# A decoder layer on one core: a rearranged head of the run, with more dense warm-up products

## The chip, the cores and the metric

The kernel runs on one core of a Trainium2 chip. The metric is the device time of one execution in microseconds, from runs of the same program; the median is compared. Of TensorE's clock two levels occur in this document, 1.2 and 2.4 GHz, called half and full.

## The reference

For one sequence of 256 tokens with 1024 channels the layer computes, all in float32:

```
mod = silu(c) @ w_ada + b_ada              # shift, scale, gate, 1024 each
h   = rmsnorm(x, norm_g) * (1 + scale) + shift
proj = h @ w_in                            # q, k, v, g_attn, cb, cc, cx, g_conv, m_attn, m_conv
attn = moba_attention(q, k, v, rel_bias)   # SEQ = MOBA_BLOCK: plain causal attention of 8 heads
y_attn = (attn * silu(g_attn)) @ w_o_attn
y_conv = (cb * conv3(cc * cx) * silu(g_conv)) @ w_o_conv
merged = sigmoid(m_attn) * y_attn + sigmoid(m_conv) * y_conv
out = rmsnorm(x + gate * (merged @ w_out), final_g)
```

Only the first two lines, and the beginning of the third, lie in the part that is changed.

## The kernel before, in words

**The head.** `x` is loaded as two tiles of 128 tokens into `xx[:, 0]` and `xx[:, 1]`, and `c` as one row, `crow`. A product with `ones` spreads `c` over 128 partitions (`pc`, L225, two products of 512 columns, contraction over one row). ScalarE and VectorE make silu(c) of it, `csb` (`silu_part`, L231). The modulation is not computed on TensorE: `w_ada` comes transposed, 128 channels to a tile `ada`, and VectorE multiplies each tile with `csb` and sums along the row (`ada_dot`, L148; the sums go to `parts`, the finished shift and scale of the 128 channels to `scs`). Meanwhile each tile of `x` is squared and summed on ScalarE (`square`, L236), `rms_scale` (L141) makes the inverse root of it (VectorE, then a power on GpSimd, `r0` and `r1`), ScalarE scales the tile, TensorE transposes it in 16 blocks of 128x128 into four banks `px` (`xn_trans`), and four copies bring them to `xnT` (`xn_copy`). `full_h(0)` (ScalarE) applies `scs` to the first 128 channels of `xnT` and gives `hf0`, the first operand of the large products.

**The stream of products.** For the k-tiles 0 to 7 (128 input channels each) `passes` (L196) multiplies a slab of `w_in` (`slab`, 2048 columns of q and k, loaded in two halves) with h, into eight banks `acc`. For k-tile 0 all 16 products are native float32, `hf0` by `slab0`, two records in the trace each. For the later ones slab and h are mostly split into a high and a low part of a faster type (`slab1h`, `slab1l`, `H`) by ScalarE and VectorE, and three products take the place of one native one. From there on the kernel goes through v, attention, convolution, gates and output in the same manner.

**What sets the order.** Nearly every instruction of the head is pinned in program order (`pin`), so each engine works its list strictly from top to bottom, and a wait holds up everything behind it on that engine. Loads go out on one queue, SyncE's, in the order of the code; the small `vecs` (norm_g, biases) and `onehot` loads go out on GpSimd's. `warm(n)` (L137) issues n products of 128x128 `ones` by `ones` whose result nobody reads.

Of the kernel before, what the change touches and what calls it, by code (L numbers as in the profile page):

```python
# [23 lines left out]
EPS = 1e-6
NEG = -1.0e30
BLK = {n: i * D for i, n in enumerate(("q", "k", "v", "ga", "cb", "cc", "cx", "gc", "ma", "mc"))}
WARM = 4
WARM2 = 6
EARLYC = 2
HALF = 8  # L30
AHEAD = 3
VCUT = 640
NATIVES = [16, 4, 2, 2, 2, 2, 2, 0]
CUTS0 = (0, 2, 3, 4)
CUTS = (0, 2, 4)
UNITS = ([("ada", i) for i in range(KT)] + [("gate", i) for i in range(4)]
         + [("v", n, kh) for n in range(2) for kh in range(2)]
# [6 lines left out]
def layer_kernel(ctx: ExitStack, tc, x, c, vec, wp_all, slab_all, onehot, final_g, out):  # L44
    nc = tc.nc
    x, out = x[0], out[0]

    const = ctx.enter_context(tc.tile_pool(name="const", bufs=1))
    big = ctx.enter_context(tc.tile_pool(name="big", bufs=1))
    wp = ctx.enter_context(tc.tile_pool(name="wp", bufs=3))  # L50
    tp = ctx.enter_context(tc.tile_pool(name="tp", bufs=2))
# [25 lines left out]
    pin = tc.keep_in_program_order  # L77
# [4 lines left out]
    xx = big.tile([P, 4, D], F32, tag="GA", name="xx")  # L82
    xnT = big.tile([P, KT, S], F32, tag="BI", name="xnT")
    csb = big.tile([P, D], F32, tag="AG", name="csb")
    crow = big.tile([1, D], F32, tag="GB", name="crow")
    vecs = const.tile([56, P], F32, name="vecs")
    oneh = const.tile([32, 3 * P + NH], F32, name="oneh")
    ident = const.tile([P, P], F32, name="ident")
    ones = const.tile([P, P], F32, name="ones")
    mhalf = const.tile([P, 1], F32, name="mhalf")  # L90
    vT = const.tile([P, 56], F32, name="vT")
    rv = const.tile([NH, 3 * P], F32, name="rv")
    scs = const.tile([P, KT, 2], F32, name="scs")
    parts = const.tile([P, KT, 2, 5], F32, name="parts")
# [18 lines left out]
            load_ada(i + 1, CUTS)  # L113
        load_slab(i, 1)

    pin(nc.sync.dma_start(crow, c))
    pin(nc.sync.dma_start(xx[:, 0, :], x[0:P, :]))
    pin(nc.sync.dma_start(xx[:, 1, :], x[P:2 * P, :]))
    load_ada(0, CUTS0)
    for h in range(2):  # L120
        load_slab(0, h)
    load_ada(1, CUTS)
    for i in range(1, AHEAD):
        load_ktile(i)
# [5 lines left out]
    nc.gpsimd.dma_start(oneh, onehot)  # L130
    nc.gpsimd.memset(rv[:, 0:127], NEG)
    warmup = const.tile([P, 1], F32, name="warmup")
    pin(nc.scalar.activation(warmup, mhalf, AF.Sigmoid))

    wt = bank("wt")

    def warm(n):  # L137
        for _ in range(n):
            pin(nc.tensor.matmul(wt[:, 0:P], ones, ones, start=True, stop=True))  # L139

    def rms_scale(ss, name):  # L141
        ms = tp.tile([P, 1], F32, tag="ms", name=name + "m")
        pin(nc.vector.tensor_scalar(ms, ss, 1.0 / D, EPS, op0=ALU.mult, op1=ALU.add))
        r = tp.tile([P, 1], F32, tag="rs", name=name + "r")
        nc.gpsimd.tensor_tensor(r, ms, mhalf, op=ALU.pow)
        return r
# [63 lines left out]
    def xn_trans(t, k):  # L210
        c0 = (k % 2) * S + t * P
        pin(nc.tensor.transpose(px[k // 2][:, c0:c0 + P], xx[:, 2 + t, k * P:(k + 1) * P], ident))

    def xn_copy(g):
        dst = xnT[:, 2 * g:2 * g + 2, :].rearrange("p a b -> p (a b)")
        if g % 2 == 0:
            pin(nc.scalar.activation(dst, px[g], AF.Copy))
        else:
            pin(nc.vector.tensor_copy(dst, px[g]))

    ss = tp.tile([P, 2], F32, name="ss")
    warm(WARM)
    pc = [bank(f"pc{n}") for n in range(2)]
    for n in range(2):
        pin(nc.tensor.matmul(pc[n], ones[0:1, :], crow[:, n * 512:(n + 1) * 512], start=True, stop=True))  # L225
    pv = bank("pv")
    pin(nc.tensor.transpose(pv[:, 0:56], vecs, ident[0:56, 0:56]))
    px = [bank(f"px{g}") for g in range(4)]
# [2 lines left out]
    def silu_part(n):  # L231
        cols = slice(n * 512, (n + 1) * 512)
        pin(nc.scalar.activation(csb[:, cols], pc[n], AF.Sigmoid))
        pin(nc.vector.tensor_mul(csb[:, cols], csb[:, cols], pc[n]))

    def square(t):  # L236
        pin(nc.scalar.activation(xx[:, 2 + t, :], xx[:, t, :], AF.Square, accum_out=ss[:, t:t + 1]))

    silu_part(0)
    square(0)  # L240
    r0 = rms_scale(ss[:, 0:1], "r0")
    pin(nc.vector.tensor_copy(vT, pv[:, 0:56]))
    modb = vT[:, 8:24].rearrange("p (k s) -> p k s", s=2)
    pin(nc.vector.scalar_tensor_tensor(modb[:, :, 1], modb[:, :, 1], 1.0, vT[:, 0:KT], op0=ALU.add, op1=ALU.mult))
    pin(nc.vector.tensor_copy(parts[:, :, :, 4], modb))
    silu_part(1)
    square(1)
    dot = ada_dot(0, CUTS0, 256)
    run(dot, EARLYC)
    r1 = rms_scale(ss[:, 1:2], "r1")  # L250
    run(dot)
    pin(nc.scalar.activation(xx[:, 2, :], xx[:, 0, :], AF.Copy, scale=r0))
    for k in range(2):
        xn_trans(0, k)
# [202 lines left out]
    n = 0  # L457
    for j in range(4):
# [7 lines left out]
        for t in range(2):  # L466
# [102 lines left out]

    def finish(t, ms, cols, src=None):  # L570
        r = tp.tile([P, 1], F32, tag="rs", name=f"rf{t}")
        nc.gpsimd.tensor_tensor(r, ms, mhalf, op=ALU.pow)  # L572
        pregain(t, cols, src)
        nc.vector.tensor_scalar_mul(TT[:, t, 0:VCUT], TT[:, t, 0:VCUT], r)
        nc.sync.dma_start(out[t * P:(t + 1) * P, 0:VCUT], TT[:, t, 0:VCUT])
        nc.scalar.activation(TT[:, t, VCUT:], TT[:, t, VCUT:], AF.Copy, scale=r)
        nc.scalar.dma_start(out[t * P:(t + 1) * P, VCUT:], TT[:, t, VCUT:])

    for n in range(2):
# [10 lines left out]
        else:  # L590
# [5 lines left out]
            ms = tp.tile([P, 1], F32, tag="ms", name="ms0")  # L596
# [78 lines left out]
```

## Time and profile before

| what | us |
|---|---|
| median of 3 runs | 329.48 |
| lowest, highest | 328.32, 330.96 |
| profiled execution, span from first to last instruction | 329.4 |
| TensorE busy | 321.4 (98%) |
| VectorE busy | 247.3 (75%) |
| ScalarE busy | 189.0 (57%) |

For the profiled execution the page gives no time beside its span. Times in the rows are microseconds from the start of the span, durations "mean" or min/median/max in ns. PE is TensorE, PEld its loads of the stationary operand, DVE VectorE, ACT ScalarE, POOL GpSimd, SPq SyncE's queue of loads. The column PEclk is the granted clock as a share of full speed. It needs care here: the trace holds a first clock record some 19 us after the start, and ahead of it the column stands at 1.00 whatever the clock was.

### The profile page before, as it was taken

Reading aid. Unit: us, or ns where it says so; the run is one execution under the profiler, and the core shown is the slowest. Engines: PE = TensorE matmul, PEld = TensorE weight load, DVE = VectorE, ACT = ScalarE, POOL = GpSimd, SP = SyncE. Lnnn points to the kernel's source line nnn. Section 1 sums busy time; section 2 is a strip of 40 time slices with the busy share of each in tenths; the row PEclk is TensorE's granted clock in tenths of the full one; section 3 lists DMA queues with packets and bytes.
Section 4 is the critical chain, followed back from the end, with each engine's and each line's share of the span. In section 5 each row is a group of like instructions: output and inputs, shape, how many; then the busy total and the mean of one; then the engine's idle time right before and its main releaser. Section 6 shows DMA issues by size and latency. Waiting matters only on the chain.

```text
span 329.4 us, 4903 instructions
## 1 busy us (share of the span) xinstructions
PE 321.4 (98%) x1870; PEld 281.9 (86%) x1870; DVE 247.3 (75%) x452; ACT 189.0 (57%) x305; POOL 5.6 (2%) x14
## 2 busy tenths in 40 slices
PE   8999999999999999999999999999999999999992
PEld 5689999988888888988888888888888888888892
DVE  2799993476388779697776998999946466787764
ACT  5654555364578676784768574856465635443430
POOL 3000000000000000000000000000000000000010
PEclk9999999999999999999999999999999999999998
DMA  6999999885645434543454469659875665400003
GB/s 240 406 409 403 410 412 352 309 303 214 247 150 200 171 129 141 211 160 127 137 206 169 142 217 373 225 193 370 346 294 205 228 218 202 182 0 2 0 0 127
DMA packets 14264, 72.75 MB, mean 221 GB/s; under 512 B 1523, under 2 KB 2819, under 8 KB 8098
## 3 DMA queue, kind: packets, MB, share of 16 engines
q1 hardware_dynamic: 12658, 70.40, 57.4%
q10 hardware_dynamic: 1488, 1.97, 1.9%
q8 instruction: 14, 0.23, 0.3%
q0 software_dynamic: 96, 0.09, 0.1%
q14 instruction: 8, 0.07, 0.1%
HBM read 71.39 MB, written 1.06 MB: 220 GB/s over the span
## 4 chain that ended last, share of the span: by engine, by line
PE 93%; DMA 2%; DVE 2%; ACT 1%; POOL 1%; SPq 0%; issue 0%; POOLq 0%; DVEq 0%; ACTq 0%
PE acc L205 15%; PE aoa L340 5%; PE acx L340 5%; PE aoc L340 5%; PE acb L340 5%; PE agc L340 5%; PE aga L340 4%; PE amc L340 4%; PE ama L340 4%; PE acc L340 4%; PE aoc L341 2%; PE aoa L341 2%; PE acx L341 2%; PE acc L341 2%; PE acb L341 2%; PE amc L341 2%
## 5 line engine op out<-in xcount | busy, mean ns | idle before, releaser
L205 PE MATMUL acc<-hf,slab 128*128 128x256 f32 x60 | 16.1, 418 | 0.0
L205 PEld LDWEIGHTS acc<-hf,slab 128*128 128x128 f32 x60 | 12.2, 213 | 3.0 <-ACT H L270 1.3
L155 DVE CUSTOM_DVE_ANT_0 ada<-ada,csb,vT 128x512 f32<-128x512 f32 (+1 forms) x18 | 12.3, 687 | 0.0
L155 DVE CUSTOM_DVE_ANT_0 ada<-ada,csb 128x512 f32<-128x512 f32 (+1 forms) x18 | 11.2, 626 | 0.5 <-DMA ada<-in_wp_dram 0.5
L407 DVE CUSTOM_DVE_ANT_0 L<-pS,BI 128x128 f32<-128x128 f32 x8 | 2.3, 292 | 12.2 <-PE pS L404 12.2
L306 DVE TENSOR_SCALAR QK<-acc 128x512 f32<-128x512 f32 x2 | 1.4, 686 | 9.1 <-PE acc L205 9.1
L572 POOL TENSOR_TENSOR rf<-ms,mhalf 128x1 f32<-128x1 f32 x2 | 1.7, 826 | 306.1 <-DVE ms L597 302.5
L554 ACT ACTIVATE SQ<-TT 128x512 f32<-128x512 f32 x3 | 1.9, 626 | 7.6 <-DVE TT L549 7.6
L304 ACT ACTIVATE QK<-acc 128x512 f32<-128x512 f32 x4 | 2.2, 601 | 7.0 <-PE acc L205 7.0
L377 DVE CUSTOM_DVE_ANT_0 gate<-gate,csb,vT 128x512 f32<-128x512 f32 x8 | 6.0, 744 | 0.3 <-DMA gate<-in_wp_dram 0.3
L139 PE MATMUL wt<-ones 128*128 128x128 f32 x20 | 5.0, 437 | 1.0 <-DVE parts L127 1.0
L340 PE MATMUL aoa<-GA,oa0h 128*128 128x512 f32 x16 | 5.8, 404 | 0.0
L340 PE MATMUL aoa<-GA,oa1h 128*128 128x512 f32 x16 | 5.7, 399 | 0.0
L340 PE MATMUL aoc<-GC,oc2h 128*128 128x512 f32 x16 | 5.7, 399 | 0.0
L340 PE MATMUL aoc<-GC,oc1h 128*128 128x512 f32 x16 | 5.7, 399 | 0.0
L340 PE MATMUL aoa<-GA,oa3h 128*128 128x512 f32 x16 | 5.7, 399 | 0.0
L340 PE MATMUL acx<-H,cx0h 128*128 128x512 f32 x16 | 5.7, 398 | 0.0
L340 PE MATMUL aoc<-GC,oc0h 128*128 128x512 f32 x16 | 5.7, 398 | 0.0
L340 PE MATMUL aoa<-GA,oa2h 128*128 128x512 f32 x16 | 5.7, 398 | 0.0
L340 PE MATMUL aoc<-GC,oc3h 128*128 128x512 f32 x16 | 5.7, 398 | 0.0
L340 PE MATMUL acc<-H,cc0h 128*128 128x512 f32 x16 | 5.7, 398 | 0.0
L340 PE MATMUL acb<-H,cb0h 128*128 128x512 f32 x16 | 5.7, 398 | 0.0
(460 smaller groups left out, 1221.9 us busy)
## 6 DMA issues: line engine op xcount, KB each, us to landing
slab<-in_slab_dram SPq DMA_DIRECT2D x16, 512.0 KB, 10.2
ada<-in_wp_dram SPq DMA_DIRECT2D x15, 512.0 KB, 10.2
wv<-in_wp_dram SPq DMA_DIRECT2D x4, 1024.0 KB, 10.6
wcc<-in_wp_dram SPq DMA_DIRECT2D x4, 1024.0 KB, 4.8
wcx<-in_wp_dram SPq DMA_DIRECT2D x4, 1024.0 KB, 4.8
wcb<-in_wp_dram SPq DMA_DIRECT2D x4, 1024.0 KB, 4.8
wgc<-in_wp_dram SPq DMA_DIRECT2D x4, 1024.0 KB, 4.8
wga<-in_wp_dram SPq DMA_DIRECT2D x4, 1024.0 KB, 4.9
```

Source lines behind the costliest of these rows:

```text
L139: pin(nc.tensor.matmul(wt[:, 0:P], ones, ones, start=True, stop=True))
L155: pin(nc.vector.tensor_tensor_reduce(src, src, csb[:, k:k + n], vT[:, i:i + 1] if s else 1.0, 0.0, ALU.mult, ALU.add, parts[:, i, s, k // ...
L205: pin(nc.tensor.matmul(acc[j // 2][:, (j % 2) * S:(j % 2 + 1) * S], w[i][:, j * P:(j + 1) * P], x, start=(i == 0 and j // 2 not in opened) ...
L304: pin(nc.scalar.activation(dst, src, AF.Copy, scale=scale))
L306: pin(nc.vector.tensor_scalar_mul(dst, src, scale))
L340: nc.tensor.matmul(a, hi[:, k, cols], rhs[:, k, :], start=(k == 0), stop=False)
L341: nc.tensor.matmul(a[:, S:], lo[:, k, cols], rhs[:, k, 0:S], start=False, stop=(k == KT - 1))
L377: nc.vector.tensor_tensor_reduce(src, src, csb[:, q * 512:(q + 1) * 512], 1.0, 0.0 if q else vT[:, 24 + b:25 + b], ALU.mult, ALU.add, gpar ...
L407: nc.vector.tensor_tensor_reduce(L[:, 0:P], pS[:, 0:P], BI[:, h, 0:P][:, ::-1], 1.0, -3.0e38, ALU.add, ALU.max, mx[:, 0:1])
L554: nc.scalar.activation(SQ[:, t, 0:w], TT[:, t, cols], AF.Square, accum_out=s8[:, slot:slot + 1])
L572: nc.gpsimd.tensor_tensor(r, ms, mhalf, op=ALU.pow)
```

## The change

- Loads: `x` tile 0, then `c`, then `x` tile 1 (before: `c`, `x`, `x`). `crow` becomes a tile of 128 rows that is zeroed first (its first half on VectorE, its second on GpSimd), and `c` is loaded into row 0 behind that. The product that spreads `c` contracts over 128 rows.
- The first `ada` tile is loaded in two parts, not three, and its dots have 512 columns (4 of them), not 256 (8).
- Warm-up products: 11 at the beginning (before 4), 6 in the middle as before, and 6 new ones right ahead of the first product with `slab0`.
- Squares: tile 0 stays on ScalarE, and comes ahead of the first sigmoid; tile 1 goes to VectorE. Both sums then go through one scale and one power operation of two columns (`r01`).
- The copy of `vT` moves from VectorE to ScalarE; the three small operations on `modb` and `parts` move to GpSimd.
- The product with `onehot` has 258 columns, not 384, and comes between the transposes. The transposes of tile 0 and 1 alternate. `xn_copy(1)` moves from VectorE to ScalarE, and `xn_copy(1)` and `(2)` stand ahead of `full_h(0)`.

```diff
-WARM = 4
+WARM = 11
 WARM2 = 6
-EARLYC = 2
+WARM3 = 6
-CUTS0 = (0, 2, 3, 4)
+CUTS0 = (0, 2, 4)
...
-    crow = big.tile([1, D], F32, tag="GB", name="crow")
+    crow = big.tile([P, D], F32, tag="GB", name="crow")
-    mhalf = const.tile([P, 1], F32, name="mhalf")
+    mhalf = const.tile([P, 2], F32, name="mhalf")
...
-    pin(nc.sync.dma_start(crow, c))
     pin(nc.sync.dma_start(xx[:, 0, :], x[0:P, :]))
+    nc.vector.memset(ones, 1.0)
+    nc.gpsimd.memset(crow[:, 512:], 0.0)
+    pin(nc.vector.memset(crow[:, 0:512], 0.0))
+    pin(nc.sync.dma_start(crow[0:1, :], c))
     pin(nc.sync.dma_start(xx[:, 1, :], x[P:2 * P, :]))
...
-        if g % 2 == 0:
+        if g < 3:
             pin(nc.scalar.activation(dst, px[g], AF.Copy))
...
-        pin(nc.tensor.matmul(pc[n], ones[0:1, :], crow[:, n * 512:(n + 1) * 512], start=True, stop=True))
+        pin(nc.tensor.matmul(pc[n], ones, crow[:, n * 512:(n + 1) * 512], start=True, stop=True))
...
+    pin(nc.scalar.activation(xx[:, 2, :], xx[:, 0, :], AF.Square, accum_out=ss[:, 0:1]))
     silu_part(0)
-    square(0)
-    r0 = rms_scale(ss[:, 0:1], "r0")
-    pin(nc.vector.tensor_copy(vT, pv[:, 0:56]))
+    pin(nc.vector.tensor_tensor_reduce(xx[:, 3, :], xx[:, 1, :], xx[:, 1, :], 1.0, 0.0, ALU.mult, ALU.add, ss[:, 1:2]))
+    ms2 = tp.tile([P, 2], F32, tag="ms2", name="ms2", bufs=1)
+    pin(nc.vector.tensor_scalar(ms2, ss, 1.0 / D, EPS, op0=ALU.mult, op1=ALU.add))
+    r01 = tp.tile([P, 2], F32, tag="r01", name="r01", bufs=1)
+    pin(nc.gpsimd.tensor_tensor(r01, ms2, mhalf, op=ALU.pow))
+    silu_part(1)
+    pin(nc.scalar.activation(vT, pv[:, 0:56], AF.Copy))
     modb = vT[:, 8:24].rearrange("p (k s) -> p k s", s=2)
-    pin(nc.vector.scalar_tensor_tensor(modb[:, :, 1], modb[:, :, 1], 1.0, vT[:, 0:KT], op0=ALU.add, op1=ALU.mult))
-    pin(nc.vector.tensor_copy(parts[:, :, :, 4], modb))
-    silu_part(1)
-    square(1)
-    dot = ada_dot(0, CUTS0, 256)
-    run(dot, EARLYC)
-    r1 = rms_scale(ss[:, 1:2], "r1")
-    run(dot)
-    pin(nc.scalar.activation(xx[:, 2, :], xx[:, 0, :], AF.Copy, scale=r0))
+    pin(nc.gpsimd.tensor_scalar_add(modb[:, :, 1], modb[:, :, 1], 1.0))
+    pin(nc.gpsimd.tensor_mul(modb[:, :, 1], modb[:, :, 1], vT[:, 0:KT]))
+    pin(nc.gpsimd.tensor_copy(parts[:, :, :, 4], modb))
+    run(ada_dot(0, CUTS0, 512))
+    pin(nc.scalar.activation(xx[:, 2, :], xx[:, 0, :], AF.Copy, scale=r01[:, 0:1]))
     for k in range(2):
         xn_trans(0, k)
+    pb = wt[0:NH, P:512]
+    pin(nc.tensor.matmul(pb[:, 126:], oneh[:, 3 * P:], oneh[:, 126:3 * P], start=True, stop=True))
...
     xn_copy(0)
     for k in range(2, KT):
-        xn_trans(0, k)
-    for k in range(2, KT):
-        xn_trans(1, k)
-    pb = wt[0:NH, P:512]
-    pin(nc.tensor.matmul(pb, oneh[:, 3 * P:], oneh[:, 0:3 * P], start=True, stop=True))
+        for t in range(2):
+            xn_trans(t, k)
+    xn_copy(1)
+    xn_copy(2)
+    warm(WARM3)
     full_h(0)
-    xn_copy(1)
     xn_copy(3)
-    xn_copy(2)
```

How the lists of the engines read at three places. First TensorE from the beginning to the first product of the stream (`wt<-ones` is a warm-up product, `px` a transpose, `pv` the transpose of `vecs`); before:

```order
L139 MATMUL wt<-ones 128x128 x4
L225 MATMUL pc_131<-crow,ones 128x512
L225 MATMUL pc_132<-crow,ones 128x512
L227 MATMUL pv<-ident,vecs 128x56
L139 MATMUL wt<-ones 128x128 x6
L212 MATMUL px_137<-ident,xx 128x128 x4
L212 MATMUL px_138<-ident,xx 128x128 x2
L212 MATMUL px_139<-ident,xx 128x128 x2
L212 MATMUL px_140<-ident,xx 128x128 x2
...
L212 MATMUL px_140<-ident,xx 128x128 x2
L265 MATMUL wt<-oneh 8x384
L205 MATMUL acc_206<-hf_194,slab_95 128x256 x2
```

and now:

```order
L141 MATMUL wt<-ones 128x128 x11
L220 MATMUL pc_139<-crow,ones 128x512
L220 MATMUL pc_140<-crow,ones 128x512
L222 MATMUL pv<-ident,vecs 128x56
L141 MATMUL wt<-ones 128x128 x6
L207 MATMUL px_145<-ident,xx 128x128 x2
L249 MATMUL wt<-oneh 8x258
L207 MATMUL px_145<-ident,xx 128x128 x2
L207 MATMUL px_146<-ident,xx 128x128 x4
...
L207 MATMUL px_148<-ident,xx 128x128 x4
L141 MATMUL wt<-ones 128x128 x6
L200 MATMUL acc_213<-hf_203,slab_97 128x256 x2
```

The product that spreads `c` now stands behind 11 warm-up products, and six more stand between the last transpose and the stream.

Second, VectorE from its first wait on (`r0m`, `r1m` and `ms` are the sums of squares, scaled; ISA rows are the dots and their reads of the sum); before:

```order
L234 TENSOR_TENSOR csb<-csb,pc_131 128x512
L143 TENSOR_SCALAR r0m<-ss 128x1
L242 COPY vT<-pv 128x56
L244 SCALAR_TENSOR_TENSOR vT<-vT 128x8
L245 COPY parts<-vT 128x16
L234 TENSOR_TENSOR csb<-csb,pc_132 128x512
L155 ISA ada_91,parts<-ada_91,csb 128x256
```

and now:

```order
L229 TENSOR_TENSOR csb<-csb,pc_139 128x512
L233 ISA xx,ss<-xx 128x1024
L233 ISA ss 128x1
L235 TENSOR_SCALAR ms_159<-ss 128x2
L229 TENSOR_TENSOR csb<-csb,pc_140 128x512
L150 ISA ada_94,parts<-ada_94,csb 128x512
```

The square of `x` tile 1 stands behind the first half of `csb`, and the scale of both tiles behind that square.

Third, ScalarE from the scaling of `x` tile 0 on (`hf` is `full_h(0)`); before:

```order
L252 ACTIVATE xx<-xx,r0r 128x1024
L255 ACTIVATE xx<-xx,r1r 128x256
L258 ACTIVATE xx<-xx,r1r 128x768
L217 ACTIVATE xnT<-px_137 128x512
L165 ACTIVATE hf_194<-xnT,scs 128x256
L217 ACTIVATE xnT<-px_139 128x512
```

and now:

```order
L245 ACTIVATE xx<-xx,r_161 128x1024
L250 ACTIVATE xx<-xx,r_161 128x256
L253 ACTIVATE xx<-xx,r_161 128x768
L212 ACTIVATE xnT<-px_145 128x512
L212 ACTIVATE xnT<-px_146 128x512
L212 ACTIVATE xnT<-px_147 128x512
L160 ACTIVATE hf_203<-xnT,scs 128x256
```

`hf` now has two more copies ahead of it on its engine.

## Rows read from the trace of the kernel before

**Rows 1.** The page: busy time, share of the span, instructions

```profile
PE 321.4 (98%) x1870; PEld 281.9 (86%) x1870; DVE 247.3 (75%) x452; ACT 189.0 (57%) x305; POOL 5.6 (2%) x14
```

**Rows 2.** Chain of waits, first 17 us: start, duration, what

```profile
2.00 6.81 DMA ada<-in_wp_dram
...
8.84 0.42 DVE ada L155
...
9.77 0.73 POOL r1r L145
...
10.52 0.52 ACT xx L255
...
11.08 3.25 PE px L212 x14
14.33 1.37 PE wt L265 x2
15.70 1.58 PE acc L205 x3
```

**Rows 3.** Timeline of the head, PE: start, duration, line, operation

```profile
1.04 2.08 PE L139 MATMUL wt<-ones 128*128 128x128 f32 x8 [1.04 <-DVE parts L127]
...
3.05 3.78 PE L225 MATMUL pc<-crow,ones 1*128 1x512 f32 x4
...
7.04 2.93 PE L139 MATMUL wt<-ones 128*128 128x128 f32 x12
...
9.76 0.63 PE L212 MATMUL px<-ident,xx 128*128 128x128 f32 x2
...
15.63 9.05 PE L205 MATMUL acc<-hf,slab 128*128 128x256 f32 x32
...
24.34 1.30 PE L205 MATMUL acc<-H,slab1h 128*128 128x256 f32 x8
```

**Rows 4.** Line L205, windows 17.2 to 18.7 and 20 to 24: ns, starts

```profile
L205 PE MATMUL acc<-hf,slab x5: 634/634/634, 16.6 to 18.4; 128*128 128x256 f32 x5
...
L205 PE MATMUL acc<-hf,slab x20: 379/379/379, 19.8 to 23.9; 128*128 128x256 f32 x20
```

**Rows 5.** Stretches at the end: length, busy by engine, PEclk, DMA

```profile
315.00:323.20 8.20, 8.16 (x59) 7.57 (x57) 5.58 (x16) 1.93 (x5) 0.93 (x1) 1.00 0.13 50
323.20:326.60 3.40, 0.00 (x0) 0.00 (x0) 1.89 (x6) 0.61 (x1) 0.72 (x1) 1.00 0.13 49
326.70:329.40 2.70, 0.00 (x0) 0.00 (x0) 0.00 (x0) 0.00 (x0) 0.00 (x0) 0.50 0.43 160
```

**Rows 6.** Timeline of the head, ACT, DVE and POOL

```profile
0.73 0.20 POOL masks.py:197 MEMSET ident<- 128x128 f32 x1 [0.29 <-POOLq L664]
...
0.82 0.17 DVE L125 MEMSET ones<- 128x128 f32 x1 [0.82 <-PEq L664]
...
5.16 0.60 ACT L233 ACTIVATE csb<-pc 128x512 f32<-128x512 f32 x1 [2.94 <-PE pc L225]
...
5.79 0.69 DVE L234 TENSOR_TENSOR csb<-csb,pc 128x512 f32<-128x512 f32 x1 [4.75 <-ACT csb L233]
...
7.06 0.56 POOL L145 TENSOR_TENSOR r0r<-r0m,mhalf 128x1 f32<-128x1 f32 x1 [4.01 <-DVE r0m L143]
...
8.40 1.14 ACT L252 ACTIVATE xx<-xx,r0r 128x1024 f32<-128x1024 f32 x1
...
12.03 0.16 DVE L158 TENSOR_REDUCE scs<-parts 128x2 f32<-128x10 f32 x1
...
12.44 0.60 ACT L165 ACTIVATE hf<-xnT,scs 128x256 f32<-128x256 f32 x1
...
15.31 0.69 DVE L155 CUSTOM_DVE_ANT_0 ada<-ada,csb 128x512 f32<-128x512 f32 x1
...
19.32 0.42 DVE L175 TENSOR_TENSOR H<-hf,H 128x256 fp32r<-128x256 f32 x1
```

**Rows 7.** Timeline of the head, SP's queue

```profile
1.54 0.42 SPq L118 DMA_DIRECT2D xx<-in_x_dram  x1
```

More of the change, by code (lines that the diff above doesn't have):

```diff
@@ L124, in layer_kernel @@
         load_ktile(i)
-    nc.vector.memset(ones, 1.0)
     nc.vector.memset(mhalf, -0.5)
@@ L132, in layer_kernel @@
     warmup = const.tile([P, 1], F32, name="warmup")
-    pin(nc.scalar.activation(warmup, mhalf, AF.Sigmoid))
+    pin(nc.scalar.activation(warmup, mhalf[:, 0:1], AF.Sigmoid))
     wt = bank("wt")
@@ L139, in warm @@
             pin(nc.tensor.matmul(wt[:, 0:P], ones, ones, start=True, stop=True))
[L141 to L146, printed above, removed]
     def ada_dot(i, cuts, n):
@@ L234, in silu_part @@
         pin(nc.vector.tensor_mul(csb[:, cols], csb[:, cols], pc[n]))
-    def square(t):
-        pin(nc.scalar.activation(xx[:, 2 + t, :], xx[:, t, :], AF.Square, accum_out=ss[:, t:t + 1]))
+    pin(nc.scalar.activation(xx[:, 2, :], xx[:, 0, :], AF.Square, accum_out=ss[:, 0:1]))
     silu_part(0)
-    square(0)
-    r0 = rms_scale(ss[:, 0:1], "r0")
-    pin(nc.vector.tensor_copy(vT, pv[:, 0:56]))
-    modb = vT[:, 8:24].rearrange("p (k s) -> p k s", s=2)
-    pin(nc.vector.scalar_tensor_tensor(modb[:, :, 1], modb[:, :, 1], 1.0, vT[:, 0:KT], op0=ALU.add, op1=ALU.mult))
@@ L253, in layer_kernel @@
     for k in range(2):
         xn_trans(0, k)
-    pin(nc.scalar.activation(xx[:, 3, 0:256], xx[:, 1, 0:256], AF.Copy, scale=r1))
+    pb = wt[0:NH, P:512]
+    pin(nc.tensor.matmul(pb[:, 126:], oneh[:, 3 * P:], oneh[:, 126:3 * P], start=True, stop=True))
+    pin(nc.scalar.activation(xx[:, 3, 0:256], xx[:, 1, 0:256], AF.Copy, scale=r01[:, 1:2]))
     for k in range(2):
         xn_trans(1, k)
-    pin(nc.scalar.activation(xx[:, 3, 256:], xx[:, 1, 256:], AF.Copy, scale=r1))
+    pin(nc.scalar.activation(xx[:, 3, 256:], xx[:, 1, 256:], AF.Copy, scale=r01[:, 1:2]))
@@ L571, in finish @@
         r = tp.tile([P, 1], F32, tag="rs", name=f"rf{t}")
-        nc.gpsimd.tensor_tensor(r, ms, mhalf, op=ALU.pow)
+        nc.gpsimd.tensor_tensor(r, ms, mhalf[:, 0:1], op=ALU.pow)
         pregain(t, cols, src)
```

## The prediction

> **What bounds the kernel now.** I read the page first, then the chain of waits, then the timeline of the first 25 us, then single lines in narrow windows. On the page TensorE is busy for 98% of the span [rows 1], so a microsecond counts only if it reaches TensorE's list. The chain of waits [rows 2] shows where that list begins to decide: up to 8.84 the first `ada` tile's load is waited for, then come a dot, the power for `r1`, the scaling of `x` tile 1, and from 11.08 on TensorE alone: transposes, the `onehot` product, and from 15.70 the stream. From there the kernel is TensorE's to its tail. Two things in the head can therefore move the end: when the stream's first product starts, and how fast the first products run.
>
> How fast: the same product record takes 634 ns in the starts from 16.6 to 18.4 and 379 ns from 19.8 on [rows 4]. By starts, that is four steps in 1.8 us (0.45 each) and 19 steps in 4.1 us (0.216 each), the half and the full level, 1.2 and 2.4 GHz. So the clock was still at half 3 us into the stream; the column PEclk says nothing of it, since no record precedes that rise. The 32 records of k-tile 0 reach from 15.63 to 24.34, 8.71 us [rows 3]; at full level they would be 32 x 0.216 = 6.9 us. **1.8 us are lost to the half level**, and that is the largest thing this change can touch.
>
> What TensorE did before the rise: dense products without a break from 15.63 to about 19.1, the middle of 18.4 and 19.8, thus for 3.5 us (2.8 to 4.2). What had not raised it for the stream: 2.0 us of warm-up products, 3.8 us of products over a single row, 2.7 us of warm-up products, and transposes [rows 3]. What makes it fall is seen once, at the end: no product after 323.2, granted 1.00 up to 326.6, 0.50 from 326.7 on [rows 5].
>
> **The change, step by step**, on the clock of the profiled execution. A 128-column record costs 2.72 / 12 = 0.227 at half (the 12 records from 7.04 to 9.76 [rows 3]) and half of 0.216, 0.108, at full.
>
> *Warm-up and c.* TensorE starts at 1.04 as before, behind the memset of `ones`. Eleven products are 22 x 0.227 = 5.0 us, so the list reaches `pc` at 6.0 at half level, where it was at 3.05. The products over 128 rows follow, so dense work lasts from 1.04 on. If the clock rises as soon as in the stream, it does at 4.5 (1.04 + 3.5); if it takes twice that, at 8.0. I take the middle, 6.3. The two `pc` products took 3.78 us [rows 3], 1.89 each: 0.3 at half and (1.89 - 0.3) / 2 = 0.8 give the first at 7.1, the second at 8.1. The first `csb` sigmoid, at 5.16 before [rows 6], is thus 2 us later.
>
> *The loads.* The load of `c` now waits for both memsets, and `x` tile 1, `ada` and the slabs queue behind it on SP. No row has a memset of 512 columns; four times the 128-column ones are 0.68 on VectorE and 0.80 on GpSimd [rows 6], so `c` issues at 1.5 to 1.6 and `x` tile 1 at 2.0, where it was issued at 1.54 [rows 7]: 0.4 later for everything behind. Cover: `x` tile 1 is now read at 8.4, `ada`, there by 8.8 before, at 10.7. Without this cover it would cost those 0.4. GpSimd's own loads shift by at most 0.8 behind the memset; `pv` now comes at 8 instead of 6.8, and hides it.
>
> *The scale.* ScalarE has squared tile 0 long before. From 7.1: sigmoid 0.60 and multiply 0.69 [rows 6] give 8.4. The square of tile 1 on VectorE has no row of its kind with 1024 columns; a dot of 256 takes 0.42 and one of 512 takes 0.69 [rows 2, 6], so 0.27 for each 256 more, 1.2 here (bounds 0.7 and 1.4). With the read and the scale, 0.3, it is 9.9; the power took 0.56 and 0.73 [rows 2, 6], so 10.6. Tile 0 is scaled 1.14 later, 11.7; this scaling began at 8.40 before. Tile 1 follows with 0.5 and 0.9, until 13.1.
>
> *Transposes and copies.* Two transposes, the `onehot` product (1.37 us for 384 columns [rows 2], so 0.46 for 258 at full level) and two transposes fit between 11.8 and 12.9. ScalarE, free at 13.1, then does three copies at 0.6 (the price of a 512-column pass [rows 6]) and `hf` at 0.6, where it had one copy ahead: 13.1 + 1.8 + 0.6 = 15.5, against 13.04 before. The two extra copies, 1.2 us, are on the path. TensorE does the other 12 transposes from 13.1 in 1.3 and the six new products in 1.3: 15.7.
>
> *What is hidden.* Four dots of 0.69 instead of eight shorter ones start at 10.6 behind the second `csb` half and end `scs` at 13.4 (12.2 before); `hf` asks for it at 14.9. GpSimd's three small operations, at most 3 x 0.73 after 10.6, end at 12.8, ahead of that sum. k-tile 1: its last operand was ready at 19.74 [rows 6], 4.6 us before its products at 24.34. The dots that lead to it began at 15.31; now they wait for `hf`, `H` and the low part, 16.4, so it is ready at 20.8, still ahead.
>
> **Sum.** The stream starts at 15.7, as it did; with the clock at full it ends k-tile 0 at 15.7 + 6.9 = 22.6, where the next begins at 24.34: 1.7 us gained, 0.1 of it left for a semaphore's way: 1.6. The span of 329.4, near the median of 329.48, becomes 327.8. Bounds: with the clock up at 4.5 the scale chain moves 0.9 earlier, 326.9, and with a shorter square and power 326.5; with the rise at 8.0 and the dear square 328.8.
>
> **Rival one, slower: the clock falls back among the transposes.** The middle warm-up ends at about 9.7; the next dense products come at 14.4. In these 4.7 us TensorE has only 16 transposes and the small product. In the rows, 3.4 us without any product ended in a granted clock of 0.50 [rows 5]. If transposes count for little, the clock falls near 13.2. The last 12 then take 2.7 and end at 15.9, the six products 2.7 more, to 18.6; the rise comes 3.5 after 15.9 at the earliest, 19.4, or a middle 20.0, so the stream loses 0.4 to 0.7. 18.6 + 0.7 + 6.9 = 26.2: 1.9 slower than 24.34, 331.3 (330.4 to 332.5). The point that decides is the level of the last transposes. For it: the transposes before the stream left the clock at half [rows 3, 4]. Against it: that they don't raise it does not say that they let it fall, and the idle stretch of rows 5 held no work at all.
>
> The Trainium skill, "TensorE: Matmul & The Clock Gate", Part 4 on the transpose, says that transposes don't count as work for the clock the way products do, which speaks against this change; the rows agree as far as the rise goes, and for the fall no row shows it.
>
> **Rival two: the gain is eaten by the path.** `r01` joins both tiles, so tile 0 waits for tile 1's square, and `hf` has two more copies ahead. If the engines' handoffs cost 0.2 each over the eight steps from `pc` to `hf`, the stream starts at 17.3, and what the clock gives is spent: 329.4.
>
> **Rival three: the clock does not rise at all ahead of the stream**, because zero rows of `crow` or the gap in front of `pc` count as a break. All at half: `pc` at 7.9, `hf` at 16.8, the transposes done at 17.0, the six products at 19.7, the rise at 20.5 or later: 19.7 + 0.5 + 6.9 = 27.1, 2.8 slower, 332.2.
>
> **Chances.** Forecast 0.55; rival one 0.27, since the open question is a single one and the rows lean only a little; rival two 0.11; rival three 0.07. What a measurement of this kernel tells from no change is about 1%, 3.3 us; the three runs before reach from 328.32 to 330.96. No case gains 3.3 us by its own sum: 0.08 for faster, from the best ends together with a lucky set of runs. Slower by over 3.3 us are the far ends of rivals one and three: 0.08. Within 1%: 0.84. For 8 in 10 the range takes the forecast's bounds, rival two and the nearer half of rival one: 326.3 to 331.6; the forecast alone is 326.5 to 328.8.
>
> **What the profile after would show.** Right: the warm-up records' distance drops from 0.23 to 0.11 us before or within `pc`, the six products ahead of the stream take 1.3 us in all, every `hf,slab` record takes about 379 ns, the stream starts at 15.2 to 16.3 and `slab1h` begins at 22 to 23.3. Rival one: a fall of the granted clock at 11 to 14.5, and `hf,slab` records of 634 ns again. Rival two: full level, start beyond 17. What would make me wrong altogether: a k-tile after the first that waits for VectorE, which moves the gain back, or a `c` load that lands after 6.0.

## The result: 0.85% slower, and the profile after

Before 329.55 us (20 runs, 327.02 to 333.15), after 331.68 (20 runs, 330.46 to 333.23): ratio 1.0085 (95%: 1.0063 to 1.0107). This ratio, like all below, leaves out runs over 1.5% above the fastest of their kernel (3 of before's 20, none of after's); the medians of all runs differ by 0.65%. The forecast of 327.8 was 3.9 too low, and the time lies 0.1 above the range. The profiled execution of after took 330.78, the fourth fastest of its 20, with a span of 328.9.

The page of after, and its chain of waits (start, duration, what), which answer to [rows 1, 2]:

```profile
PE 319.3 (97%) x1896; PEld 283.1 (86%) x1896; DVE 247.2 (75%) x442; ACT 188.8 (57%) x305; POOL 7.0 (2%) x17
```

```profile
5.91 0.88 PE pc L220 x2
...
6.81 0.61 ACT csb L228
...
8.13 1.17 DVE xx L233
...
9.60 0.73 POOL r L237
...
10.36 1.16 ACT xx L245
...
11.56 0.44 PE px L207 x2
11.99 0.53 PE wt L249 x2
12.52 3.18 PE px L207 x14
15.70 1.45 PE wt L141 x12
17.16 0.87 PE acc L200 x4
```

Up to the first transpose at 11.56 the chain is the predicted one, a little early. Then 14 transposes take 3.18 us, and six new products stand between them and the stream. The timeline of PE says what came ahead, answering to [rows 3] (the last bracket of a row is the idle time before it and what ended it), and a view by stretches gives the granted clock (length; busy us of PE, PEld, DVE, ACT, POOL; PEclk; DMA share; GB/s):

```profile
1.04 4.87 PE L141 MATMUL wt<-ones 128*128 128x128 f32 x22 [1.04 <-DVE ones L117]
5.75 1.88 PE L220 MATMUL pc<-crow,ones 128*128 128x512 f32 x4
...
7.76 1.60 PE L141 MATMUL wt<-ones 128*128 128x128 f32 x12
11.56 0.44 PE L207 MATMUL px<-ident,xx 128*128 128x128 f32 x2 [2.20 <-ACT xx L245]
...
12.45 3.25 PE L207 MATMUL px<-ident,xx 128*128 128x128 f32 x14
15.50 1.66 PE L141 MATMUL wt<-ones 128*128 128x128 f32 x12
...
23.72 1.30 PE L200 MATMUL acc<-H,slab1h 128*128 128x256 f32 x8
```

```profile
11.60:12.30 0.70, 0.70 (x4) 0.25 (x4) 0.67 (x3) 0.70 (x2) 0.23 (x1) 1.00 1.06 433
12.45:15.50 3.05, 3.05 (x16) 3.05 (x15) 0.88 (x5) 2.09 (x5) 0.00 (x0) 0.50 1.02 416
...
15.90:17.00 1.10, 1.10 (x13) 1.10 (x12) 1.08 (x3) 0.49 (x2) 0.00 (x0) 1.00 1.03 410
```

Twelve warm-up records in 1.60 us tell of the full level by 7.76; TensorE then waits 2.20 us for ScalarE's scaling, works at full level to 12.30, and is at half from 12.45 to 15.50. From 15.90 it is full again. The stream's products, which answer to [rows 4], all run at full level, by the view of line L200 from 17 to 24 us (ns min/median/max, starts):

```profile
L200 PE MATMUL acc<-hf,slab x32: 379/379/382, 17.0 to 23.7; 128*128 128x256 f32 x32
```

K-tile 1 begins at 23.72, 0.6 earlier than in the profiled execution of before [rows 3]. Yet the change is slower. So the two profiled executions can't both be typical.

**What further traces show.** The table has one line for each trace of this study; the first five kernels are before unchanged, the next four after unchanged, the others are the experiments below. "Pause" is TensorE's longest wait between 6 and 16 us; "full" and "fall" are the changes of the granted clock, by its records in the trace (all but the last fall, behind the last product); "rest" is the span less the start of k-tile 1.

| trace | pause | full | fall | full again | stream | k-tile 1 | rest | span |
|---|---|---|---|---|---|---|---|---|
| before | 0.69 | 19.47 | | | 15.63 | 24.34 | 305.1 | 329.4 |
| before_again | 1.38 | 15.84 | | | 16.11 | 22.93 | 305.1 | 328.0 |
| before_look | 1.70 | 10.12 | | | 14.44 | 21.26 | 305.1 | 326.4 |
| before_look2 | 1.44 | 19.94 | | | 16.39 | 24.95 | 305.1 | 330.1 |
| before_19 | 0.46 | 11.47 | | | 13.54 | 20.37 | 305.1 | 325.5 |
| after | 2.20 | 5.58 | 12.41 | 15.82 | 17.00 | 23.72 | 305.2 | 328.9 |
| after_look1 | 2.16 | 5.42 | 12.25 | 15.66 | 16.88 | 23.60 | 306.5 | 330.1 |
| after_look2 | 2.16 | 4.11 | 10.94 | 17.76 | 17.85 | 24.57 | 306.5 | 331.1 |
| after_fill | 2.16 | 7.01 | 13.84 | 17.25 | 17.70 | 24.42 | 306.8 | 331.2 |
| after_warm4 | 1.68 | 8.74 | 12.16 | 15.57 | 17.04 | 23.76 | 306.8 | 330.6 |
| after_nowarm3 | 2.16 | 6.86 | 13.69 | 17.10 | 16.06 | 23.38 | 306.5 | 329.9 |
| after_nowarm3_hf | 2.16 | 6.58 | 13.41 | 16.82 | 15.53 | 22.90 | 306.8 | 329.7 |
| after_oldload | 0.24 | 9.86 | | | 14.03 | 20.75 | 306.5 | 327.3 |
| after_cqueue | 0.97 | 9.84 | | | 15.93 | 22.66 | 306.5 | 329.2 |
| after_eq | 1.60 | 8.75 | | | 15.05 | 21.87 | 306.5 | 328.4 |
| after_fill16 | 0 | 4.99 | | | 15.06 | 21.78 | 306.5 | 328.3 |
| before_gap | 0.99 | 10.22 | | | 13.83 | 20.65 | 305.1 | 325.8 |
| before_early | 0 | 11.59 | | | 13.13 | 19.95 | 305.1 | 325.1 |
| before_cuts | 0.41 | 10.87 | | | 13.23 | 20.05 | 305.2 | 325.2 |
| before_tiles | 0.53 | 12.03 | | | 13.86 | 20.68 | 304.4 | 325.0 |

Three things stand in it. One kernel, before, has its clock full anywhere between 10.1 and 19.9 us, and its spans of 328.0 and more go with a rise at 15.8 or later. After has a fall among the transposes in 4 of 4 traces. And the rest of the run is 1.4 to 1.7 longer in 10 of the 11 traces of kernels with the change, in none of the 9 without.

### The profile page after: what moved, and what is told of

Same layout as the page of the kernel before. It is cut to its first block, busy times and chain, and to the rows that moved or that the text cites. A ratio compares the mean times of both kernels' runs of the same rounds, so it can differ in the third digit from the quotient of the medians.

```text
span 328.9 us, 4947 instructions
## 1 busy us (share of the span) xinstructions
PE 319.3 (97%) x1896; PEld 283.1 (86%) x1896; DVE 247.2 (75%) x442; ACT 188.8 (57%) x305; POOL 7.0 (2%) x17
## 4 chain that ended last, share of the span: by engine, by line
PE 95%; issue 1%; DVE 1%; ACT 1%; POOL 1%; POOLq 0%; ACTq 0%
PE acc L200 15%; PE aoc L333 5%; PE aoa L333 5%; PE acx L333 5%; PE acc L333 5%; PE acb L333 5%; PE aga L333 5%; PE amc L333 5%; PE ama L333 5%; PE agc L333 4%; PE aoc L334 2%; PE aoa L334 2%; PE acb L334 2%; PE acx L334 2%; PE acc L334 2%; PE agc L334 2%
## 5 line engine op out<-in xcount | busy, mean ns | idle before, releaser
L200 PE MATMUL acc<-hf,slab 128*128 128x256 f32 x60 | 14.1, 379 | 0.0
L150 DVE CUSTOM_DVE_ANT_0 ada<-ada,csb,vT 128x512 f32<-128x512 f32 x16 | 11.9, 746 | 0.0
L200 PEld LDWEIGHTS acc<-hf,slab 128*128 128x128 f32 x60 | 10.9, 190 | 1.2
L150 DVE CUSTOM_DVE_ANT_0 ada<-ada,csb 128x512 f32<-128x512 f32 x16 | 11.0, 685 | 0.3 <-DMA ada<-in_wp_dram 0.3
L141 PE MATMUL wt<-ones 128*128 128x128 f32 x46 | 8.1, 350 | 1.0 <-DVE ones L117 1.0
L141 PEld LDWEIGHTS wt<-ones 128*128 128x128 f32 x46 | 7.8, 264 | 1.1 <-DVE ones L117 1.0
L207 PE MATMUL px<-ident,xx 128*128 128x128 f32 x16 | 3.7, 409 | 2.2 <-ACT xx L245 2.2
L333 PE MATMUL acc<-H,cc3h 128*128 128x512 f32 x16 | 5.8, 403 | 0.0
L229 DVE TENSOR_TENSOR csb<-csb,pc 128x512 f32<-128x512 f32 x2 | 1.4, 683 | 5.9 <-ACT csb L228 5.9
```

The source lines that it names most:

```text
L200: pin(nc.tensor.matmul(acc[j // 2][:, (j % 2) * S:(j % 2 + 1) * S], w[i][:, j * P:(j + 1) * P], x, start=(i == 0 and j // 2 not in opened) ...
L333: nc.tensor.matmul(a, hi[:, k, cols], rhs[:, k, :], start=(k == 0), stop=False)
```

## The experiments

**Before again, and after again.** No edit. First a repetition with 12 runs, then single executions, each traced.

> The kernel before, run again for the span, clock and trace of further executions. Theory A (late start): an ordinary execution of before has its clock up earlier than the one profiled execution I read, so its time minus its span is about 1.8 us as in the changed kernel (330.78 against 328.9), its spans lie around 327.7, and a new trace has the first-stage products at 379 ns from earlier than 19 us. Theory C (outside the span): time and span agree within 0.3 us, the spans are about 329.4, and the 2 us of the change lie outside the span.

> One more execution of the kernel before, for its trace; half of its spans so far lie at 325 to 326.5, a third at 329.3 to 330.1, some at 328. Theory A (the clock's rise is what differs): a span near 325.5 comes with a rise before 15 us and a stream that runs at 379 ns throughout and starts by 14.5; a span near 329.5 with a rise 3 to 4 us into the stream, as in the trace I predicted from. Theory D (the loads differ): the stream's clock is the same and the first ada part lands 2 to 4 us apart.

> One more execution of the kernel before. Theory E: some executions have the slow rest of 306.5. Theory F: 305.1 again, and the span is set by when the clock rises: 325.5 to 326.5 with a rise before 15, 329.4 with one near 19.

> One more execution of the kernel before, a sixth trace. Theory G and H: rest 305.1, units of 5.20. Theory E (each execution falls into a rhythm by chance): a slow rest is due among six if chance alone decides. The span follows the clock's rise: 325 to 326.5 with a rise near 10, about 328 near 15.8, 329.4 and more near 19.

> One more execution of the changed kernel, for its trace. So far each trace splits into the time at which the second k-tile begins and the rest, and the rest has been 305.1 to 305.2 us or 306.5 to 306.8 us; in the second kind the products of the gates' units go 2% slower, 5.30 us a unit for 5.20, at the same granted clock. Theory E (the rhythm falls anew in each execution): some executions of the changed kernel have the slow rest, others not. Theory F (the rhythm hangs on the program): the changed kernel always has the fast rest, 305.2, and its longer spans come from the head alone, with the second k-tile beginning at 24 to 26.

> As the look before it. Theory B (the clock falls in the pause ahead of the transposes) expects a fall between 9 and 14.5 us in this trace too, whatever the rest of the kernel does.

> One more execution of the changed kernel, a third trace, under the same expectation: a fall of the clock ahead of the stream; the second k-tile at 23.5 or later.

before_19 and after_fill, too, are before and after without an edit; no pause is filled in them. before_again: 328.84 (326.78 to 333.37, 12 runs), ratio 0.9972 (0.9927 to 1.0018), the measure of what two equal kernels differ by. The single executions of before took 328.16, 331.84 and 327.26, those of after 332.00, 332.89 and 333.01. Line L205 in two executions of before, answering to [rows 4], the first two rows of before_look2, then one of before_19:

```profile
L205 PE MATMUL acc<-hf,slab x6: 634/634/794, 16.4 to 18.7; 128*128 128x256 f32 x6
...
L205 PE MATMUL acc<-hf,slab x24: 379/379/380, 20.0 to 24.9; 128*128 128x256 f32 x24
```

```profile
L205 PE MATMUL acc<-hf,slab x31: 379/379/483, 13.5 to 20.1; 128*128 128x256 f32 x31
```

The loss that the change was to take away is in the first trace and absent from the second. Over 106 runs of before in this study 51 spans lie in 324 to 326.8, 23 from there to 328.9 and 32 above; of after's 20 none is below 328.7.

**Fewer warm-up products.** after_warm4 has 4 at the beginning; after_nowarm3 leaves out those ahead of the stream; after_nowarm3_hf also restores the old order of the copies, the second one back on VectorE; after_eq takes 4 at the beginning and none ahead of the stream.

```diff
# after_warm4, after_eq
-WARM = 11
+WARM = 4
# after_nowarm3, after_nowarm3_hf, after_eq
-    warm(WARM3)
# after_nowarm3_hf as well
-        if g < 3:
+        if g % 2 == 0:
-    xn_copy(1)
-    xn_copy(2)
     full_h(0)
+    xn_copy(1)
     xn_copy(3)
+    xn_copy(2)
```

> The changed kernel with 4 warm-up products at the beginning, not 11. Theory A (late start): the product that spreads c begins at about 4 instead of 5.7, the scale chain and with it hf come about 1 us earlier, the stream starts 0.7 to 1.2 us earlier: 330.5 to 331.0, ratio to before 1.003 to 1.006. Theory B (clock): the seven products were what raised the clock; without them it rises later, spreading c and the transposes go at half level, the stream starts no earlier and partly at half: 332 or more, ratio 1.008 or more.

> The changed kernel without the six products ahead of the stream. Theory A (late start): they are 1 us of the path; the stream starts when hf is ready, at 16.0 instead of 17.0, at full level: 330.7, ratio 1.005. Theory B (clock): they are what keeps or raises the clock for the stream; without them the first 2 to 4 us of the stream run at half: 331.7 to 332.7, ratio 1.008 to 1.011.

> As the kernel without the six products, and with the copies and hf in the order of before (hf right behind the first copy, the second copy back on VectorE). Theory A (late start): hf is 1.2 us earlier, ready at 14.8, so that the last transposes, done at 15.5, bound the stream: start 15.6, 330.3, ratio 1.003 or less. Theory B (clock): the earlier start is one at half level, and the gain over the kernel without the six products is under 0.5 us.

> The changed kernel with 4 warm-up products at the beginning and none ahead of the stream, so that TensorE's list up to the gates is as long as in the kernel before. Theory G (the place in TensorE's list sets the slow rhythm): units of the gates back at 5.20, rest 305.1 to 305.2; the head is the changed one, second k-tile at 22.5 to 24, time 329.7 to 331, ratio 1.000 to 1.005. Theory H (something else of the change does, as the tiles' places or the order of loads): units of 5.30 and a rest of 306.5 or more, 331 to 332.5, ratio 1.005 to 1.009.

Ratios to before: 1.0041 (1.0003 to 1.0079), 1.0071 (1.0035 to 1.0108), 1.0062 (1.0027 to 1.0097), 1.0104 (1.0059 to 1.0149); none is faster. after_warm4's 330.88 is what theory A has, after_nowarm3_hf's 331.60 is later than its 330.3. In after_nowarm3 the stream's first 1.0 us (16.06 to 17.10) ran at half, not the 2 to 4 that theory B has; after_eq has the time of theory G (330.43) and the rest of theory H. The traced executions of the first three fell in clock, that of after_eq didn't, though its PE timeline is after_warm4's up to the transposes but for hundredths; first after_warm4, then after_eq:

```profile
7.95 1.97 PE L141 MATMUL wt<-ones 128*128 128x128 f32 x12
11.60 0.44 PE L207 MATMUL px<-ident,xx 128*128 128x128 f32 x2 [1.68 <-ACT xx L245]
...
12.78 3.09 PE L207 MATMUL px<-ident,xx 128*128 128x128 f32 x14
```

```profile
8.03 1.93 PE L141 MATMUL wt<-ones 128*128 128x128 f32 x12
11.57 0.44 PE L207 MATMUL px<-ident,xx 128*128 128x128 f32 x2 [1.60 <-ACT xx L245]
...
12.47 1.75 PE L207 MATMUL px<-ident,xx 128*128 128x128 f32 x14
```

The same 14 transposes take 3.09 and 1.75. That is a difference of executions, not of the two kernels, as the runs without a trace show (below). With eleven products (after) or four, the scaling starts at 10.4: with an early `pc` the chain hangs on the load of `x` tile 1 instead, as after_warm4's chain of waits has it:

```profile
1.98 6.11 DMA xx<-in_x_dram
...
8.11 1.23 DVE xx L233
...
10.40 1.16 ACT xx L245
```

**The loads.** after_oldload takes the old order `c`, `x`, `x`, without the memsets and with `pc` over one row, and 4 warm-up products; after_cqueue keeps the new loads but issues `c` on ScalarE's queue, with 4 too.

```diff
# after_oldload
+    pin(nc.sync.dma_start(crow, c))
     pin(nc.sync.dma_start(xx[:, 0, :], x[0:P, :]))
-    nc.gpsimd.memset(crow[:, 512:], 0.0)
-    pin(nc.vector.memset(crow[:, 0:512], 0.0))
-    pin(nc.sync.dma_start(crow[0:1, :], c))
...
-        pin(nc.tensor.matmul(pc[n], ones, crow[:, n * 512:(n + 1) * 512], ...
+        pin(nc.tensor.matmul(pc[n], ones[0:1, :], crow[:, n * 512:(n + 1) * 512], ...
# after_cqueue
-    pin(nc.sync.dma_start(crow[0:1, :], c))
+    pin(nc.scalar.dma_start(crow[0:1, :], c))
```

> The changed kernel with the old head of loads and the old spreading of c (c first, one row, no memsets, product over one row, 4 warm-up products); squares, merged scale, copies, dots of 512 and the six products ahead of the stream stay. Theory A1 (the load of c is what starts the stream late: x tile 1 lands at 8.05, not 5.8, and the first ada part at 10.4, not 8.8): tile 1 is squared from 6.5, the scaling begins near 9 instead of 10.4, the stream starts near 15.7 and the time is 329.5 to 330, ratio 0.999 to 1.002. Theory A2 (the merged scale and the copies start it late): no better than the changed kernel with 4 warm-up products, 330.9, ratio 1.004.

> The changed kernel with 4 warm-up products and the load of c issued by ScalarE, so that x tile 1 and ada don't queue behind its wait on SP. Theory A1 (late loads): x tile 1 lands before 6.5, ada before 9.3, the scaling begins 0.8 to 1.2 us earlier than with c on SP: 329.8 to 330.2, ratio 1.001. Theory A2 (path behind it): unchanged from 4 warm-up products with c on SP, 330.9.

PE of after_oldload:

```profile
10.21 0.44 PE L205 MATMUL px<-ident,xx 128*128 128x128 f32 x2 [0.24 <-ACT xx L243]
...
11.11 1.75 PE L205 MATMUL px<-ident,xx 128*128 128x128 f32 x14
12.69 1.50 PE L139 MATMUL wt<-ones 128*128 128x128 f32 x12
14.03 1.25 PE L198 MATMUL acc<-hf,slab 128*128 128x256 f32 x5
```

With the old loads the scaling starts at 9.00 (after: 10.36), the pause shrinks to 0.24, there is no fall, and k-tile 1 begins 3.0 earlier than in after. In after_cqueue `x` tile 1 landed at 5.25, but `c` so late that `pc` began at 5.31 and the scaling at 10.91. The times don't follow the heads, and both expectations of theory A1 were missed: 331.53 and 331.06, ratios 1.0089 (1.0056 to 1.0121) and 1.0092 (1.0059 to 1.0124). The rest is long in both. Of after_oldload's 10 spans three are 327.3 to 327.6, like the traced one, and seven 329.6 to 330.4; no trace of those seven exists, and their granted clocks, 0.994 to 0.995, tell of no fall.

**The pause filled.** after_fill16 is after with ten more products ahead of the transposes.

```diff
-WARM2 = 6
+WARM2 = 16
```

> The changed kernel with 16 warm-up products in the middle, not 6, so that TensorE has work until the first transposes. Theory B (the pause lets the clock fall): no fall ahead of the stream, transposes 0.11 us apart, not 0.21, the stream starts at 15.5 to 16.3, the second k-tile at 22.3 to 23.1, 1 to 1.5 us earlier: 330.2 to 330.9 with the slow rest, ratio to before 1.002 to 1.005. Theory I (transposes let it fall, whatever comes before): a fall all the same, second k-tile at 23.6 or later, 331.7.

Its timeline of PE and the stretch in which after was at half:

```profile
7.47 3.84 PE L141 MATMUL wt<-ones 128*128 128x128 f32 x32
11.24 0.44 PE L207 MATMUL px<-ident,xx 128*128 128x128 f32 x2
...
12.13 1.75 PE L207 MATMUL px<-ident,xx 128*128 128x128 f32 x14
13.72 1.50 PE L141 MATMUL wt<-ones 128*128 128x128 f32 x12
15.06 1.25 PE L200 MATMUL acc<-hf,slab 128*128 128x256 f32 x5
```

```profile
12.50:15.00 2.50, 2.50 (x25) 2.50 (x24) 0.80 (x2) 2.36 (x5) 0.00 (x0) 1.00 1.03 416
```

No pause and no fall, as theory B has it; k-tile 1 begins at 21.78, 1.8 to 2.8 earlier than in the four traces of after. This is one trace, but the mean granted clock that every run reports tells of the others. In the 20 traces above it is 0.986 to 0.992 where the clock fell, and 0.994 to 0.998 where it didn't. Over all runs with a clock on record:

| kernel | pause in its traces | runs at 0.992 or below |
|---|---|---|
| after, after_nowarm3, after_nowarm3_hf | 2.16 to 2.20 | 47 of 47 |
| after_warm4, after_eq | 1.68, 1.60 | 5 of 18 |
| after_cqueue, after_oldload, after_fill16 | 0.97, 0.24, 0 | 0 of 22 |
| before | 0.46 to 1.70 | 1 of 109 |

So the fall comes from the pause; in before, the clock is not always full ahead of it. In after_look2 the fall, at 10.94, came 0.12 us behind the pause, when hardly a transpose had run (the first row lies in the pause):

```profile
8.70:10.80 2.10, 0.00 (x0) 0.00 (x0) 2.10 (x7) 1.18 (x2) 1.79 (x4) 1.00 1.03 408
10.95:12.30 1.35, 1.35 (x4) 0.19 (x4) 1.14 (x5) 1.04 (x2) 0.37 (x1) 0.50 1.06 373
```

The time of after_fill16 gained less: 330.24 (330.09 to 331.04), ratio 1.0082 (1.0054 to 1.0111). In its trace the rest is 306.5.

**Small edits in the kernel before.** before_gap puts the `onehot` product, 258 columns, between the transposes; before_early puts `r1` ahead of the first dots and the product behind four transposes; before_cuts loads the first `ada` tile in two parts; before_tiles has only the tiles of another size, two spare ones among them.

```diff
# before_early; before_gap moves the product alone, behind xn_trans(0, k)
-EARLYC = 2
+EARLYC = 0
...
     for k in range(2):
         xn_trans(1, k)
+    pb = wt[0:NH, P:512]
+    pin(nc.tensor.matmul(pb[:, 126:], oneh[:, 3 * P:], oneh[:, 126:3 * P], start=True, stop=True))
...
-    pb = wt[0:NH, P:512]
-    pin(nc.tensor.matmul(pb, oneh[:, 3 * P:], oneh[:, 0:3 * P], start=True, stop=True))
# before_cuts
-CUTS0 = (0, 2, 3, 4)
+CUTS0 = (0, 2, 4)
# before_tiles
-    mhalf = const.tile([P, 1], F32, name="mhalf")
+    mhalf = const.tile([P, 2], F32, name="mhalf")
+    for n in ("ms2", "r01"):
+        spare = tp.tile([P, 2], F32, tag=n, name=n, bufs=1)
...
```

> The kernel before with one edit: the onehot product, 258 columns, stands between the first two transposes and the next, where TensorE waited for ScalarE, and no longer between the last transpose and the stream. Theory A (late start and clock): TensorE works from 7.0 to the stream without a break, so the clock rises in each execution before the stream, which starts at 13.1 to 14.3: the executions at 328 to 330 go, median 327.3, ratio to before 0.991 to 0.995. Theory D (loads differ): only the product's 1.3 us go from the path where TensorE bounds it, and the spread of 4 to 6 us between executions stays: ratio 0.996 to 0.999.

> The kernel before with two edits: the scale of x tile 1 is taken ahead of the first dots, which wait for ada, and the onehot product, 258 columns, comes right behind the first four transposes. Theory A (the head's path and the clock): tile 1 is scaled from 9.5, not 10.5 to 11.5, TensorE's pause behind the middle warm-up shrinks to 0.2 us, so that the clock is up before the stream in each execution, which starts when hf is ready, 13.1 to 14.1; second k-tile at 20 to 21, spans 325.1 to 326.1, time 327 to 328, ratio 0.991 to 0.997, and no executions over 329. Theory D (the loads set the spread): spread as before, ratio 0.997 to 1.000.

> The kernel before with the first ada tile in two loads, as the change has it, and nothing else (its dots keep 256 columns). All later loads move up by one in the rotation of the semaphores that SP's queue waits on. Theory J (this shift brings the slow rhythm): units of the gates at 5.30, rest 306.5, time 1.4 us over the kernel before in like executions. Theory H (tiles' places) and theory K (the later start itself): 5.20, rest 305.1.

> The kernel before with the change's tiles: mhalf with two columns, and two spare tiles of two columns where the change has ms2 and r01 (zeroed once, read by nobody), so that what is allocated behind them lies where it does in the changed kernel. Theory H (the tiles' places bring the slow rhythm): units at 5.30, rest 306.5. Theories J and K: 5.20, rest 305.1.

Ratios: 0.9986 (0.9953 to 1.0018), 0.9954 (0.9922 to 0.9986), 0.9975 (0.9921 to 1.0029), 0.9969 (0.9924 to 1.0014). **before_early**, 326.87 (326.35 to 328.93, 12 runs), beats both kernels, by a little more than theory A has it: its longest span is 327.2, where before's reach 331.5. before_gap's longest is 327.1, but its median did not gain as theory A has it. PE of before_early, without a pause:

```profile
7.63 2.34 PE L139 MATMUL wt<-ones 128*128 128x128 f32 x10
9.76 1.06 PE L212 MATMUL px<-ident,xx 128*128 128x128 f32 x4
10.75 0.99 PE L259 MATMUL wt<-oneh 32*8 32x258 f32 x2
11.68 1.53 PE L212 MATMUL px<-ident,xx 128*128 128x128 f32 x12
13.13 1.13 PE L205 MATMUL acc<-hf,slab 128*128 128x256 f32 x4
```

None of the four has the long rest. The difference shows in single tiles of the gates; the view of tile gc2h in after, after_look1, after_fill16 and before_early:

```profile
L333 PE MATMUL agc<-H,gc2h x16: 392/394/395, 177.3 to 182.5; 128*128 128x512 f32 x16
```

```profile
L333 PE MATMUL agc<-H,gc2h x16: 395/398/403, 177.0 to 182.3; 128*128 128x512 f32 x16
```

```profile
L333 PE MATMUL agc<-H,gc2h x16: 395/398/403, 175.2 to 180.5; 128*128 128x512 f32 x16
```

```profile
L340 PE MATMUL agc<-H,gc2h x16: 392/394/395, 173.5 to 178.7; 128*128 128x512 f32 x16
```

The same 16 products reach over 5.2 us (first to last start) in one rhythm and 5.3 in the other, both at a granted clock of 1.00. Over the units from gc2 to the last of the mixing gates this makes the 1.4. The list of instructions behind the head is the same in after and after_look1, one kernel, and they differ. after_eq has as many warm-up products as before, after_oldload the old order of loads, and both have the long rest: neither the products nor the new loads are needed for it. The cut of `ada` (before_cuts) and the tiles (before_tiles) didn't bring it in their one trace each; since after, too, has had the short rest once, one trace doesn't rule a cause out. What brings it stays open: the merged scale, the moved small operations on GpSimd and the transposes' order, for example, were not tried alone.

## Why the prediction was wrong, step by step

- **"Sum": the base was mis-read, the largest error.** Span and time were set equal ("329.4, near the median of 329.48"). In all runs here with both on record the time is 1.7 to 1.9 above the span (after: 330.78 to 328.9), so the profiled execution took about 331.2 and was one of before's slower ones. The median 329.55 means a span near 327.8, and less 305.1 k-tile 1 at 22.6 or so: just where the forecast put it after the change (22.6). "1.8 us are lost to the half level" was true of that execution; in three of the five traces of before the clock was full ahead of the stream. Even a change that worked as forecast would have measured 327.8 + 1.8 = 329.6, no gain.
- **"Sum", "with the clock at full": failed, by rival one.** The point that was to decide, the level of the last transposes, was named right, and the rival had a chance of 0.27. The fall came at 12.41 (13.2 forecast), the last transposes ended at 15.5 (15.9). Why: the forecast looked at the work among the transposes, but what decided was TensorE's wait of 2.2 us ahead of them. With it the clock fell in 47 of 47 runs; without it the same transposes ran at full (after_fill16). So the stream began at 17.0, not 15.7, and k-tile 1 at 23.7, not 22.6. The rival's price was too high (k-tile 1 at 26.2, now 23.7): it had the rise 3.5 us behind the last transpose at the earliest, and the rise came at 15.82, 0.3 behind it. The six products thus took 1.5, not 2.7, and the stream lost nothing. That the rival's 331.3 lies near the measured 331.68 is luck: its head was too dear, and it left out the 1.8 between span and time and what the rest lost.
- **Transposes and the rise.** In after and after_look1 a stretch at half that held nearly nothing but transposes (in after 12.45 to 15.5, then 0.3 us of products) was followed by full level. By the Trainium skill, "TensorE: Matmul & The Clock Gate", Part 4: PE-mode transpose, the full level doesn't engage for transposes; these two traces speak against that for the float32 blocks of 128x128 here, if they run in the mode that the page means, which the trace doesn't say. In after_look2 the transposes ran on from 10.82 and the rise came only at 17.76, so it is not shown what part of a stretch counts.
- **"Warm-up and c", "The scale": right.** `pc` at 5.75 (6.0), the clock full at 5.58 (6.3; 4.11 to 7.01 in the other traces of after), the first sigmoid at 6.81 (7.1), the square 1.23 (1.2), tile 0 scaled from 10.36 (10.6), `hf` done at 15.97 (15.5).
- **"The loads": mis-sized, and hidden by a hair.** `x` tile 1 was issued at 1.99, as forecast, but had landed at 8.05 instead of 5.80: 2.25 later, not 0.4. The square could not have begun before 8.13 anyway, because of `csb`. So the load cost nothing in after, but it holds the scaling at 10.4 as soon as `pc` is early (after_warm4), and with it the pause. The issue, which answers to [rows 7]:

```profile
1.99 0.35 SPq L121 DMA_DIRECT2D xx<-in_x_dram  x1
```

- **Rival two: not seen.** It asked for 0.2 us at each handoff; in the chain of after the pieces between `pc` and the scaling in which nothing is waited for are 0.02 to 0.07.
- **"What is hidden": right for the stream, silent on the rest.** No later k-tile gave the gain back; but in three of the four traces of after 1.4 to 1.7 us were lost far behind the change, with no wait in the records, which no step had.
- **Account.** The four traces of after have k-tile 1 at 24.1 on average, 1.5 behind a typical 22.6, and a rest of 306.3, 1.2 more: 2.7, where the medians differ by 2.1; the four are slower than after's 20 runs (mean span 330.3, against a median of 329.9). The head's part is larger than the rest's, but four traces don't give the shares more closely.

## What to carry to other kernels

Take several traces before pricing a loss that hangs on the clock, and compare the traced span with the spans of the other runs, not with their times: a span that is long among its like tells that the trace shows one of the slower cases. Here dense products ahead of a wait of 2.2 us did not keep the clock that they had raised; filling the wait did (after_fill16), and so did a short one (after_oldload). When a head gets faster and the time doesn't, compare the rest of the run, too.

## What was not expected of the hardware

- The same program had its clock full at 10.1 to 19.9 us in five traces, and spans from 325.5 to 330.1.
- A pause of 2.16 to 2.20 us behind dense products was followed by a fall in 6 of 6 traces, and the granted clocks tell of one in all 47 runs of these kernels; one of 1.68 was, 1.60 and 1.70 were not.
- With `c` between the two tiles on the queue of loads, the issue of `x` tile 1 came 0.45 us later and its landing 0.6 to 2.6 us later: 6.62 to 8.36 in nine traces, 5.73 to 5.98 in the ten with the old order. In the profiled executions the stretch from 3.50 to 5.80 moved 378 GB/s before and 191 after; whether the small load of `c` did it or the memsets' wait is not separated:

```profile
3.50:5.80 2.30, 2.30 (x4) 0.71 (x3) 0.01 (x1) 0.64 (x2) 0.00 (x0) 1.00 1.03 378
```

```profile
3.50:5.80 2.30, 2.30 (x14) 2.30 (x13) 0.00 (x0) 1.15 (x2) 0.00 (x0) 1.00 0.70 191
```

- Identical pairs of products keep one of two rhythms for a whole unit (394 or 398 ns, 5.2 or 5.3 us), at the same clock; before_tiles had a third course, with a rest of 304.4.
